# One-core S5/HGRN2/attention trunk: Toeplitz blocks of the S5 layers built through DRAM, weight loads placed by the planner, the taps' copy in a buffer of its own

## The chip, the core and the metric

The kernel runs on one core of a Trainium2 chip. The metric is the device time of one execution in microseconds (us); before the change the median of 3 runs is 1086.48 us (1085.96 to 1090.13).

## The reference, cut to what matters

Four layers run one after the other on x of 512 positions by 1024 features, in float32: S5, HGRN2, sliding-window attention, S5 again. Each is `h = h + rms_norm(branch(rms_norm(h)))`. The change touches only the two S5 layers:

```python
u, z = split(h @ w_in)                       # 1024 -> 2 x 1024
x[l,g,p] = u[l,g,h] * B[g,p,h]               # 64 groups of 16 channels, 64 complex states
s[l] = a * s[l-1] + x[l]                     # associative scan over 512 positions
y = gelu(real(C s) + d * u)
y = y * sigmoid(y @ w_glu + b_glu)
out = (y * silu(z)) @ w_out
```

## The kernel before, in words

**Scan by chunks.** The 512 positions are 64 chunks of 8, the 64 groups are 8 blocks (b = 0 to 7) of 8 groups. For a block `s5_v` makes vt (128x1024) from the parameters prm and the table ap on VectorE, with one factor (q12b) from GpSimd. `s5_taps` multiplies vt with c into kps (the impulse response within a chunk), ScalarE copies kps to kt, TensorE transposes vt (tps, copied to v) and kt (ktp), VectorE adds the skip term and gets ksb. ksb becomes the block's Toeplitz matrix toep: column block jj of it is ksb moved down, with zeros above. `s5_u` brings the projected input of the block through DRAM (ut, ub, u). `s5_core` multiplies u with v (xps), rotates by rotf, scans the 64 chunk states (r), rotates back (spre), and adds u times toep and spre times w into yps; ScalarE takes the gelu (ysb), two transposes (ytp) per pair of blocks bring y back, copied by ScalarE (y).

**Around it.** Between these steps TensorE runs the input projection (`s5_rest`, tile pj, 8 weight chunks), then the first half of the gate projection (`s5_glu_first`, also pj). In the first layer the input weights are used as they are (wraw); every other weight is split on the fly into whi (ScalarE) and wlo (VectorE), two pieces a chunk, and takes three matmuls instead of one. The gate's operand y is split in the same way into yh and yl; yl takes the buffer of the layer's input, so it waits until the input projection is over.

**Order.** `Flow` merges the S5 pieces: each piece says which engine it takes (P, V, A, and D for the SP queue), for how long by a fixed estimate, and after which marks; the earliest start goes next, and the engines then run in that written order. In the first layer, before, the weight loads are not pieces: `w_load` is called where the projection takes a chunk. wraw has 3 buffers, whi and wlo 4 each.

**The shared buffer.** In the first layer kt has the tag of q12b, one buffer: q12b of block b+1 is written after ktp of block b has read kt.

**Opening.** x comes in four loads; `norm_stats` squares and sums a row block on ScalarE, takes the root on GpSimd (rs_r, which needs the constants cst), scales into xs; `norm_xt` transposes (xtp) and copies (xf). `s5_tables` makes the tables of the first layer on VectorE, with sine and cosine on ScalarE.

Of the kernel before, what the change touches and what calls it, by code (L numbers as in the profile page):

```python
# [109 lines left out]
class Trunk:  # L110
# [152 lines left out]
    def norm_stats(self, L, tbs, h):  # L263

        nc = self.nc
        if tbs[0] == 0:
            if L == 0:
                self.x = (self.act.tile([P, KB, T], F32, tag="xh", name="xf"), None)
            else:
                self.x = (  # L270
                    self.act.tile([P, KB, T], F32R, tag="xh", name="xh"),
                    self.act.tile([P, KB, T], F32R, tag="xl", name="xl"),
                )
            self.xs = self.act.tile([P, 4, D], F32, tag="z", name="xs")
        xs = self.xs
        n = len(tbs)
        ss = self.small.tile([P, 2], F32, tag="pre_ss", name="pre_ss", bufs=2)
        for i, tb in enumerate(tbs):
            self.last_sq = nc.scalar.activation(out=xs[:, tb, :], in_=h[:, tb, :], func=AF.Square, accum_out=ss[:, i:i + 1])
        r = self.rstd(ss[:, 0:n], D, n)  # L280
        for i, tb in enumerate(tbs):
            if L == 0:

                nc.scalar.activation(out=xs[:, tb, :], in_=h[:, tb, :], func=AF.Copy, scale=r[:, i:i + 1])
            else:
                self.last_xs = nc.vector.tensor_scalar(out=xs[:, tb, :], in0=h[:, tb, :], scalar1=r[:, i:i + 1], scalar2=None, op0=ALU.mult)
# [336 lines left out]
    def s5_load(self, b, m):  # L623

        nc, s = self.nc, self.scr
        yield "D", 0.2, (m["states", b - 2],) if b > 1 else ()
# [8 lines left out]

    def s5_convs(self, i0, m):

        m["cv", 1].t = 0.0
        for c in range(2, 8):
            yield "A", 2.1, (m["cd", c - 2],) if c > 1 else ()  # L640
            yield "V", 2.6, ()
            self.w_conv(i0 + c)
            self.w_load(i0 + c + 1)
            yield m["cv", c]

    def s5_open(self, j):
# [5 lines left out]
        self.kt = None  # L652
        if j == 0:
            self.s5_params(j)
        else:
            self.s5t = {}
            self.kt = 1
# [6 lines left out]
        self.sp, self.tp, self.cp = [], [], []  # L664
        self.md = s.tile([P, 8, 64], F32, tag="mdec", name="mdec", bufs=1)
        nc.gpsimd.memset(self.md[:, :, 0:1], 0.0)
        for i in range(2):
            t = s.tile([P, 8, 8, 16], F32, tag=f"toep{i}", name="toep", bufs=1)
            nc.gpsimd.memset(t, 0.0)
            self.tp.append(t)  # L670
# [7 lines left out]
    def s5_rot(self, pr, m):  # L678
# [23 lines left out]
        for i in range(2):  # L702

            b = 2 * pr + i
            yield "D", 0.3, (m["states", b - 2],) if pr else ()
# [7 lines left out]
    def s5_v(self, j, b, m):  # L713
# [11 lines left out]
        yield "V", 1.3, (m["ap"],) + ((m["kt", b - 1],) if b and j == 0 else ())  # L725
# [26 lines left out]
    def s5_taps(self, b, m):  # L752
# [11 lines left out]
        kt = self.tab.tile([P, 2, 128], F32, tag="q12b" if self.kt is None else "kt", name="kt", bufs=1)  # L764
# [21 lines left out]
        yield "D", 0.6, (m["y", b - 2],) if b > 1 else ()  # L786
        d["toep"] = toep = self.tp[b % 2]
        for jj in range(8):
            n = (jj + 1) * 16
            nc.sync.dma_start(out=toep[128 - n:128, jj, :, :], in_=ksb[0:n].rearrange("p a g h -> p (a g) h"))  # L790
# [19 lines left out]
    def s5_u(self, b, ps, m):  # L810
# [6 lines left out]
        yield "D", 0.2, ()  # L817
# [3 lines left out]
        yield "D", 0.2, (m["y", b - 3],) if b > 2 else ()  # L821
# [79 lines left out]
    def s5_rest(self, L, ps, m):  # L901
# [5 lines left out]
        def chunk(c):  # L907
            if plain:
                return self.w_next("s5_in")
# [5 lines left out]
        for half in range(2):  # L915
            c = slice(half * 256, half * 256 + 256)
            for b in range(4):
                if half == 0 and b == 2:
                    if not plain:
                        yield "P", 0.0, (m["cv", 1],)  # L920
# [13 lines left out]
        for c in range(6):  # L934
            if not plain:
                yield "P", 0.0, (m["cv", c + 2],)
# [33 lines left out]
    def s5_glu_first(self, glu, y, i0, early, m):  # L970

        w = []
        for c in range(2):
            if early and c == 0:
                yield "A", 2.1, (m["cd", 6],)
                yield "V", 2.6, ()
                self.w_conv(i0 + 8)
                self.w_load(i0 + 9)
                continue
            yield "V", 2.6, (m["rest"],)  # L980
            self.w_conv(self.wi + c)
            self.w_load(self.wi + c + 1)
# [13 lines left out]
        for fb in range(4):  # L996
            if fb == 2:
                yield "V", 2.6, ()
                self.w_conv(self.wi)
                self.w_load(self.wi + 1)  # L1000
# [4 lines left out]
    def layer_s5(self, L):  # L1005
# [6 lines left out]
        with self.scratch("left"), self.tc.manual_schedule(engines={E.PE, E.DVE, E.Activation, E.SP}):  # L1012
# [8 lines left out]
            if j == 0:  # L1021
                flow.add(self.s5_tables(j, m), 0, 5.0)
            else:
# [482 lines left out]
    def run(self):  # L1506
        tc, nc, a = self.tc, self.nc, self.a
        self.plan_weights()
        with tc.tile_pool(name="cst", bufs=1) as self.small, \
# [16 lines left out]
            for tb in range(4):  # L1526
                nc.sync.dma_start(out=x0[:, tb, :], in_=a["x"][tb * 128:(tb + 1) * 128, :])
                if tb == 1:
                    self.w_load(0)
                    self.w_load(1)  # L1530
            for tb in range(4):
                self.norm_stats(self.layers[0], (tb,), x0)
# [128 lines left out]
```

## Time and profile before

| | |
|---|---|
| median of 3 runs | 1086.48 us |
| profiled execution, its own time | 1089.59 us |
| its span | 1087.8 us |
| PE / DVE / ACT / POOL busy | 94% / 69% / 46% / 10% of the span |
| first S5 layer (to the end of the gate projection) | about 0 to 274 us |
| last S5 layer, core blocks | about 858 to 996 us |

PE is TensorE, DVE VectorE, ACT ScalarE, POOL GpSimd, SP the engine that only issues transfers. Busy PE is not PE at its peak: a matmul counts until its modelled end, and the clock that the throttle grants is shown apart. What PE waits for, and at which clock it runs, is read from the timeline by stretches.

### The profile page before, as it was taken

How to read it: one execution, taken by the hardware profiler on the slowest of the kernel's cores; microseconds unless marked ns; L12 is line 12 of the kernel's file. 1: busy time of each engine (PE TensorE's matmuls, PEld its weight loads, DVE VectorE, ACT ScalarE, POOL GpSimd, SP SyncE). 2: the span in 40 equal slices, each digit the busy share in tenths (PEclk: the TensorE clock that was granted, in tenths of full speed). 3: DMA queues.
4: the chain of work that ended last, by engine and by line, in shares of the span. 5: the costliest groups of instructions: out<-in, count | busy, mean ns of one | idle time of the engine just before them, and what ended most of it. 6: DMA issues, size and time to landing. Idle time of an engine off the chain costs nothing.

```text
span 1087.8 us, 17048 instructions
## 1 busy us (share of the span) xinstructions
PE 1027.0 (94%) x6480; PEld 816.6 (75%) x6480; DVE 746.8 (69%) x1454; ACT 505.2 (46%) x937; POOL 104.4 (10%) x164
## 2 busy tenths in 40 slices
PE   5999995999999999999999999999999989897997
PEld 3855554777998798998978986666678867676875
DVE  6487789584689778888865664556656687754752
ACT  5234345554552314323244433588844556555531
POOL 2000000030200100000011021100002111000300
PEclk9999997999999999999999999999999999998999
DMA  6375333434432323424253354211223777634221
GB/s 236 79 207 147 96 102 96 157 112 150 149 106 64 126 83 107 156 73 144 67 188 141 97 134 115 59 58 45 79 83 132 212 189 197 205 96 161 96 97 58
DMA packets 70577, 133.31 MB, mean 123 GB/s; under 512 B 28896, under 2 KB 40032, under 8 KB 69472
## 3 DMA queue, kind: packets, MB, share of 16 engines
q1 hardware_dynamic: 65664, 119.04, 35.5%
q10 hardware_dynamic: 4832, 13.19, 3.7%
q8 instruction: 51, 0.84, 0.3%
q14 instruction: 30, 0.25, 0.1%
HBM read 100.51 MB, written 20.15 MB: 111 GB/s over the span
## 4 chain that ended last, share of the span: by engine, by line
PE 66%; DVE 14%; ACT 7%; DMA 5%; issue 5%; POOL 2%; SPq 2%; ACTq 1%; DVEq 0%; POOLq 0%
PE pj L233 27%; PE ops L248 14%; PE zps L248 4%; PE vps L248 3%; PE sps L1138 3%; DVE wlo L184 3%; PE scps L1346 3%; ACT whi L183 2%; PE aops L1382 2%; DMA rsw<-rraw 1%; PE yps L877 1%; SPq L790 1%; PE yps L875 1%; PE ptp L1377 1%; DVE sg L1067 1%
## 5 line engine op out<-in xcount | busy, mean ns | idle before, releaser
L233 PE MATMUL pj<-xh,whi 128*128 128x512 f32 (+1 forms) x496 | 179.9, 364 | 1.2 <-ACT xh L305 0.6
L184 DVE TENSOR_TENSOR wlo<-wraw,whi 128x1024 fp32r<-128x1024 f32 x116 | 144.6, 1262 | 52.4 <-ACT whi L183 45.2
L233 PE MATMUL pj<-xl,whi 128*128 128x512 f32 (+1 forms) x496 | 175.1, 354 | 2.1 <-DVE xl L311 2.1
L233 PE MATMUL pj<-xh,wlo 128*128 128x512 f32 (+1 forms) x496 | 175.4, 354 | 0.0
L183 ACT ACTIVATE whi<-wraw 128x1024 fp32r<-128x1024 f32 x116 | 120.7, 1056 | 73.2 <-PE pj L233 33.5
L233 PE MATMUL pj<-xf,wraw 128*128 128x512 f32 (+1 forms) x320 | 119.6, 524 | 0.4 <-ACT xf L305 0.4
L233 PEld LDWEIGHTS pj<-xh,whi 128*128 128x128 f32 x496 | 93.8, 190 | 17.5 <-issue 5.4
L233 PEld LDWEIGHTS pj<-xl,whi 128*128 128x128 f32 x496 | 94.4, 190 | 13.9 <-DVE xl L311 2.9
L233 PEld LDWEIGHTS pj<-xh,wlo 128*128 128x128 f32 x496 | 94.2, 190 | 13.5 <-issue 1.7
L248 PE MATMUL ops<-whi,gh 128*128 128x512 f32 x256 | 101.7, 398 | 2.7 <-ACT gh L1069 2.1
L248 PE MATMUL ops<-wlo,gh 128*128 128x512 f32 x256 | 100.7, 394 | 1.1 <-DVE wlo L184 1.0
L248 PE MATMUL ops<-whi,gl 128*128 128x512 f32 x256 | 100.5, 395 | 0.0
L233 PEld LDWEIGHTS pj<-xf,wraw 128*128 128x128 f32 x320 | 61.0, 198 | 42.1 <-issue 36.7
L248 PEld LDWEIGHTS ops<-whi,gh 128*128 128x128 f32 x256 | 48.2, 188 | 13.9 <-ACT gh L1069 3.0
L248 PEld LDWEIGHTS ops<-wlo,gh 128*128 128x128 f32 x256 | 48.2, 188 | 13.1 <-DVE wlo L184 2.7
L248 PEld LDWEIGHTS ops<-whi,gl 128*128 128x128 f32 x256 | 48.1, 188 | 11.2 <-DVE gl L1070 0.9
L233 PE MATMUL pj<-yh,whi 128*128 128x512 f32 x128 | 51.1, 399 | 0.0
L233 PE MATMUL pj<-yh,wlo 128*128 128x512 f32 x128 | 50.1, 392 | 0.0
L233 PE MATMUL pj<-yl,whi 128*128 128x512 f32 x128 | 50.1, 392 | 0.0
L354 DVE TENSOR_TENSOR yg<-ops,gpost 128x512 f32<-128x512 f32 x32 | 21.8, 687 | 38.8 <-ACT junk L352 38.8
L248 PE MATMUL vps<-wlo,xh 128*128 128x256 f32 x160 | 45.3, 283 | 0.0
L248 PE MATMUL vps<-whi,xl 128*128 128x256 f32 x160 | 45.3, 283 | 0.0
(279 smaller groups left out, 2100.4 us busy)
## 6 DMA issues: line engine op xcount, KB each, us to landing
wraw<-in_s_in SPq DMA_DIRECT2D x32, 512.0 KB, 4.7
wraw<-in_hg_in SPq DMA_DIRECT2D x32, 512.0 KB, 3.6
wraw<-in_at_in SPq DMA_DIRECT2D x20, 512.0 KB, 4.3
wraw<-in_s_glu SPq DMA_DIRECT2D x16, 512.0 KB, 3.8
wraw<-in_s_out SPq DMA_DIRECT2D x16, 512.0 KB, 3.5
hd<-h SPq DMA_DIRECT2D x6, 1024.0 KB, 4.0
prm<-in_s_bc SPq DMA_DIRECT2D x16, 256.0 KB, 3.8
ub<-ut SPq DMA_DIRECT2D x16, 256.0 KB, 3.7
```

The lines of the kernel that those rows point to most:

```text
L183: nc.scalar.activation(out=hi, in_=raw, func=AF.Copy)
L184: nc.vector.tensor_tensor(out=lo, in0=raw, in1=hi.bitcast(F32), op=ALU.subtract)
L233: self.nc.tensor.matmul(ps, lhsT=l[k // 4][:, k % 4, c], rhs=r[:, k, n0:n1], start=k == 0 and n == 0, stop=k == KB - 1 and n == len(terms) ...
L248: self.nc.tensor.matmul(ps, lhsT=l[:, k, c], rhs=r[k // per][:, k % per, :], start=k == 0 and n == 0, stop=k == KB - 1 and n == 2)
L354: nc.vector.tensor_tensor(out=yg[:, tb, f], in0=ps, in1=gp[:, f], op=ALU.mult)
L790: nc.sync.dma_start(out=toep[128 - n:128, jj, :, :], in_=ksb[0:n].rearrange("p a g h -> p (a g) h"))
L875: nc.tensor.matmul(o, lhsT=u[:, g, :], rhs=d["toep"][:, :, g, :], start=True, stop=False)
L877: nc.tensor.matmul(o, lhsT=sp[:, g, :], rhs=d["w"][:, g, :], start=False, stop=True)
L1067: nc.vector.tensor_tensor(out=sg, in0=sg, in1=y[:, k, :], op=ALU.mult)
L1138: nc.tensor.matmul(ps[:, c, :], lhsT=k[:, c * 128:c * 128 + 128], rhs=q4[:, c, :, 1, :], start=True, stop=True)
L1346: nc.tensor.matmul(ps[:, bb, lo:256], lhsT=self.q[r, 4 * p + 2 * b2 + bb, qs], rhs=self.k[r, p, ks], start=True, stop=True)
L1382: nc.tensor.matmul(ops[64 * i:64 * i + 64].rearrange("p b q -> p (b q)"), lhsT=self.v[:, n - 1 + f, kv * 64:kv * 64 + 64], rhs=pts[i][:, f ...
```

## The change

Five things change.

1. **toep**: before, eight transfers from ksb to shifted places of one of two tiles that were set to zero once. Now ksb is written once to a DRAM tile kd (240 rows of 128, the first 112 rows zero, written in the opening), and one transfer reads toep from it with overlapping rows. The two zero fills of 128x1024 on GpSimd go; a zero tile of 112x128 and two writes of it on the ACT queue come, ahead of cst.
2. **kt** takes the tag pw in the first layer (a buffer of the tables' making, free by then), and `s5_v` no longer waits for kt of the block before.
3. **Weight loads** become pieces of the planner (`s5_loads` in the first layer, a D piece after each conversion elsewhere), and D pieces have longer estimates.
4. **Opening**: row blocks 0 and 1 share one root, all scaling into xs is on VectorE; the load of chunk 1 is issued after x.
5. All this moves the planner's order in the two S5 layers; the instructions of the two layers between stand in the same order as before.

```diff
         for i, tb in enumerate(tbs):
-            if L == 0:
-
-                nc.scalar.activation(out=xs[:, tb, :], in_=h[:, tb, :], func=AF.Copy, scale=r[:, i:i + 1])
-            else:
-                self.last_xs = nc.vector.tensor_scalar(out=xs[:, tb, :], in0=h[:, tb, :], scalar1=r[:, i:i + 1], scalar2=None, op0=ALU.mult)
+            self.last_xs = nc.vector.tensor_scalar(out=xs[:, tb, :], in0=h[:, tb, :], scalar1=r[:, i:i + 1], scalar2=None, op0=ALU.mult)
 
...
         nc, s = self.nc, self.scr
-        yield "D", 0.2, (m["states", b - 2],) if b > 1 else ()
+        yield "D", 1.1, (m["states", b - 2],) if b > 1 else ()
         f = self.rot[b] = s.tile([P, 2, 512], F32, tag=f"rot{b % 2}", name="rotf", bufs=1)
...
 
+    def s5_loads(self, i0, m):
+
+        for c in range(1, 9):
+            yield "D", 1.0, (m["cd", 6],) if c == 8 else (m["cd", c - 3],) if c > 2 else ()
+            self.w_load(i0 + c)
+            yield m["cv", c]
+
     def s5_convs(self, i0, m):
...
             self.w_conv(i0 + c)
-            self.w_load(i0 + c + 1)
             yield m["cv", c]
+            yield "D", 1.0, ()
+            self.w_load(i0 + c + 1)
 
...
         self.tab = s = self.tabcm.__enter__()
-        self.kt = None
+        self.kt = ("pw", "kt")[j]
         if j == 0:
...
             self.s5t = {}
-            self.kt = 1
             for n, sh in (("ap", [P, 2, 64, 9]), ("co", [P, 2, 2, 64]), ("m8", [P, 64])):
...
             nc.sync.dma_start(out=dm[0:16, :], in_=self.a["s5_d"][j])
-        self.sp, self.tp, self.cp = [], [], []
+        self.sp, self.cp = [], []
+        if j == 0:
+            zero = s.tile([112, 128], F32, tag="t2", name="zero", bufs=1)
+            nc.gpsimd.memset(zero, 0.0)
+            self.kd = []
+            for i in range(2):
+                self.kd.append(self.dram.tile([240, 128], F32, tag=f"kd{i}", name="kd", bufs=1))
+                nc.scalar.dma_start(out=self.kd[i][0:112], in_=zero)
         self.md = s.tile([P, 8, 64], F32, tag="mdec", name="mdec", bufs=1)
...
         for i in range(2):
-            t = s.tile([P, 8, 8, 16], F32, tag=f"toep{i}", name="toep", bufs=1)
-            nc.gpsimd.memset(t, 0.0)
-            self.tp.append(t)
             t = s.tile([P, 8, 64], F32, tag=f"spre{i}", name="spre", bufs=1)
...
             b = 2 * pr + i
-            yield "D", 0.3, (m["states", b - 2],) if pr else ()
+            yield "D", 1.1, (m["states", b - 2],) if pr else ()
             f = s.tile([P, 2, 512], F32, tag=f"rot{i}", name="rotf", bufs=1)
...
         B = prm.rearrange("p k (g h) -> p k g h", h=16)
-        yield "V", 1.3, (m["ap"],) + ((m["kt", b - 1],) if b and j == 0 else ())
+        yield "V", 1.3, (m["ap"],) + ()
         t = self.s5t
...
         yield "A", 0.4, ()
-        kt = self.tab.tile([P, 2, 128], F32, tag="q12b" if self.kt is None else "kt", name="kt", bufs=1)
+        kt = self.tab.tile([P, 2, 128], F32, tag=self.kt, name="kt", bufs=1)
         nc.scalar.activation(out=kt, in_=kps, func=AF.Copy)
...
         nc.vector.tensor_tensor(out=ksb, in0=ktp[:, :, :, 0:16], in1=dmx.rearrange("p (a g) h -> p a g h", a=2), op=ALU.add)
-        yield "D", 0.6, (m["y", b - 2],) if b > 1 else ()
-        d["toep"] = toep = self.tp[b % 2]
-        for jj in range(8):
-            n = (jj + 1) * 16
-            nc.sync.dma_start(out=toep[128 - n:128, jj, :, :], in_=ksb[0:n].rearrange("p a g h -> p (a g) h"))
+        yield "D", 0.5, (m["toep", b - 2],) if b > 1 else ()
+        kd = self.kd[b % 2]
+        nc.sync.dma_start(out=kd[112:240], in_=ksb.rearrange("p a g h -> p (a g h)"))
+        yield "D", 0.5, (m["y", b - 2],) if b > 1 else ()
+        d["toep"] = toep = self.tab.tile([P, 8, 8, 16], F32, tag=f"toep{b % 2}", name="toep", bufs=1)
+
+        src = bass.AP(tensor=kd.tensor, offset=kd.offset, ap=[[128, P], [16 * 128, 8], [1, 128]])
+        nc.sync.dma_start(out=toep.rearrange("p j g h -> p j (g h)"), in_=src)
         yield m["toep", b]
...
         yield m["ev", b]
-        yield "D", 0.2, ()
+        yield "D", 0.5, ()
         ub = self.dram.tile([8, 128, 64], F32, tag="ub", name="ub", bufs=8)
...
         yield m["ub", b]
-        yield "D", 0.2, (m["y", b - 3],) if b > 2 else ()
+        yield "D", 0.5, (m["y", b - 3],) if b > 2 else ()
         u = s.tile([P, 8, 64], F32, tag="u", name="u", bufs=3)
...
             if plain:
-                return self.w_next("s5_in")
+                self.w_conv(self.wi)
             return self.w_take()
...
                 if half == 0 and b == 2:
-                    if not plain:
-                        yield "P", 0.0, (m["cv", 1],)
+                    yield "P", 0.0, (m["cv", 1],)
                     w.append(chunk(1))
...
         for c in range(6):
-            if not plain:
-                yield "P", 0.0, (m["cv", c + 2],)
+            yield "P", 0.0, (m["cv", c + 2],)
             w = chunk(c + 2)
...
                 self.w_conv(i0 + 8)
+                yield "D", 1.0, ()
                 self.w_load(i0 + 9)
...
             yield "V", 2.6, (m["rest"],)
-            self.w_conv(self.wi + c)
-            self.w_load(self.wi + c + 1)
+            self.w_conv(i0 + 8 + c)
+            yield "D", 1.0, ()
+            self.w_load(i0 + 9 + c)
         for c in range(2):
...
                 self.w_conv(self.wi)
+                yield "D", 1.0, ()
                 self.w_load(self.wi + 1)
...
                 flow.add(self.s5_tables(j, m), 0, 5.0)
+                flow.add(self.s5_loads(i0, m), 60)
             else:
...
                     self.w_load(0)
-                    self.w_load(1)
-            for tb in range(4):
-                self.norm_stats(self.layers[0], (tb,), x0)
+            for tbs in ((0, 1), (2,), (3,)):
+                self.norm_stats(self.layers[0], tbs, x0)
             for _ in self.norm_xt(self.layers[0], (0, 1)):
```

**Order on TensorE, first layer, from ktp of block 0 to kps of block 1.** Before:

```order
L779 MATMUL ktp<-cst,kt 128x128 x2
L233 MATMUL pj<-xf,wraw 128x512
L838 MATMUL xps<-u,v 64x64 x16
L233 MATMUL pj<-xf,wraw 128x512 x10
L762 MATMUL kps<-vt,c_92 32x128 x8
```

After:

```order
L786 MATMUL ktp<-cst,kt 128x128 x2
L233 MATMUL pj<-xf,wraw 128x512 x2
L848 MATMUL xps<-u,v 64x64 x16
L233 MATMUL pj<-xf,wraw 128x512 x3
L769 MATMUL kps<-vt,c_94 32x128 x8
L233 MATMUL pj<-xf,wraw 128x512
```

Between the two blocks stood 11 steps of the projection (one of 512 columns each), now 5. So it goes on: the last block's xps, which stood behind the whole projection, now has 8 steps of it behind it, and the yps of blocks 6 and 7 and both ytp follow, before the gate projection.

**Order on ScalarE in the opening**, up to the cosine. Before:

```order
L279 ACTIVATE xs,pre_ss<-x_98 128x1024
L447 ACTIVATE lam<-lam 128x96
L279 ACTIVATE xs,pre_ss<-x_98 128x1024
L454 ACTIVATE mag<-lrdt 128x64
L434 ACT_TABLE_LOAD
L434 ACTIVATE sin<-th 128x96
L437 ACTIVATE cos<-red_n,cst 128x96
L284 ACTIVATE xs<-x_98,rs_r 128x1024 x2
L305 ACTIVATE xf<-xtp,gpre 128x256 x2
```

After:

```order
L279 ACTIVATE xs,pre_ss<-x_100 128x1024 x2
L443 ACTIVATE lam<-lam 128x96
L450 ACTIVATE mag<-lrdt 128x64
L279 ACTIVATE xs,pre_ss<-x_100 128x1024
L301 ACTIVATE xf<-xtp,gpre 128x256 x2
L279 ACTIVATE xs,pre_ss<-x_100 128x1024
L301 ACTIVATE xf<-xtp,gpre 128x256 x4
L430 ACT_TABLE_LOAD
L430 ACTIVATE sin<-th 128x96
L301 ACTIVATE xf<-xtp,gpre 128x256 x2
L433 ACTIVATE cos<-red_n,cst 128x96
```

The scalings have left ScalarE; sine and cosine now stand behind six and eight copies of xf.

**Order on ScalarE at the end of the first layer's projection**, from the gelu of a block's yps (ysb) on; z is the last copy of the projection. Before, from ysb of block 6:

```order
L883 ACTIVATE ysb<-yps 128x4x8x16
L773 ACTIVATE v<-tps 128x512
L183 ACTIVATE whi<-wraw 128x1024 x2
L963 ACTIVATE yh<-y 128x512
L843 ACTIVATE xsw<-xps 64x512
L844 ACTIVATE xsw<-xps 64x512
L856 ACTIVATE rsw<-r 64x512
L857 ACTIVATE rsw<-r 64x512
L883 ACTIVATE ysb<-yps 128x4x8x16
L1065 ACT_TABLE_LOAD
```

After, from ysb of block 6 too:

```order
L893 ACTIVATE ysb<-yps 128x4x8x16
L961 ACTIVATE z<-pj 128x512
L971 ACTIVATE yh<-y 128x512 x2
L183 ACTIVATE whi<-wraw 128x1024 x2
L971 ACTIVATE yh<-y 128x512
L893 ACTIVATE ysb<-yps 128x4x8x16
L1077 ACT_TABLE_LOAD
L1077 ACTIVATE sz<-z 128x512
L906 ACTIVATE y<-ytp 128x4x128 x2
L1502 DMA h<-in_x 128x4x1024
L971 ACTIVATE yh<-y 128x512
L183 ACTIVATE whi<-wraw 128x1024 x2
```

The first whi pair here is the gate's chunk 0, the second its chunk 1. The core steps that stood between (v, xsw, rsw) are over by now, and chunk 1 stands behind both copies of y.

## Rows read from the trace of the kernel before

**Rows 1.** Stretches: length, busy us by engine, clock, DMA share, GB/s

```profile
120.00:160.00 40.00, 39.28 (x255) 21.10 (x254) 30.98 (x40) 16.19 (x27) 2.32 (x4) 1.00 0.37 95
...
160.00:200.00 40.00, 27.89 (x236) 19.95 (x234) 36.24 (x44) 20.37 (x32) 1.35 (x2) 0.83 0.34 92
```

**Rows 2.** Timeline of PE, first layer: start, length, instruction, [idle before]

```profile
20.84 11.03 PE L233 MATMUL pj<-xf,wraw 128*128 128x256 f32 x40 [0.40 <-ACT xf L305]
...
47.22 0.65 PE L762 MATMUL kps<-vt,c 128*32 128x128 f32 x16
...
164.73 0.64 PE L762 MATMUL kps<-vt,c 128*32 128x128 f32 x16
...
183.20 1.08 PE L762 MATMUL kps<-vt,c 128*32 128x128 f32 x16 [9.11 <-DVE vt L748]
...
191.07 0.48 PE L233 MATMUL pj<-yh,whi 128*128 128x512 f32 x1
...
200.96 0.44 PE L875 MATMUL yps<-toep,u 128*64 128x128 f32 x4 [1.43 <-DMA toep<-ksb]
```

**Rows 3.** Projection matmuls (L233) between two kps: stretch, length, PE busy, PEld busy

```profile
125.32:144.98 19.66, 13.39 (x31) 5.47 (x30) 1.00 0.33 81
```

**Rows 4.** Timeline of DVE, first layer

```profile
9.75 0.29 DVE L462 TENSOR_TENSOR ap<-mag,cos 128x64 f32<-128x64 f32 x1 [0.77 <-ACT cos L437]
...
32.43 1.22 DVE L748 TENSOR_TENSOR vt<-vt,t 128x1024 f32<-128x1024 f32 x1
...
54.79 0.29 DVE L785 TENSOR_TENSOR ksb<-ktp,dmx 128x128 f32<-128x128 f32 x1 [9.41 <-PE ktp L779]
```

**Rows 5.** Chain that ended last, its opening: start, length

```profile
1.64 6.95 DMA cst<-in_const
...
10.85 1.14 ACT xs L284
```

**Rows 6.** Line 286: the scaling on VectorE elsewhere, ns min/median/max

```profile
L286 DVE TENSOR_SCALAR xs<-h,rs_r x4: 747/752/1717, 270.2 to 293.9; 128x1024 f32<-128x1024 f32 x4
```

**Rows 7.** Timeline of ACT, first layer

```profile
12.97 0.84 ACT L305 ACTIVATE xf<-xtp,gpre 128x256 f32<-128x256 f32 x2 [0.99 <-PE xtp L301]
...
168.26 0.60 ACT L883 ACTIVATE ysb<-yps 128x512 f32<-128x512 f32 x1 [1.89 <-PE yps L877]
...
169.60 1.11 ACT L896 ACTIVATE y<-ytp 128x512 f32<-128x512 f32 x1 [0.17 <-PE ytp L892]
...
170.50 2.01 ACT L183 ACTIVATE whi<-wraw 128x1024 fp32r<-128x1024 f32 x2
...
203.58 1.28 ACT L1065 ACT_TABLE_LOAD   x1
```

**Rows 8.** PE in one stretch of the last layer: busy, clock

```profile
950.00:954.00 4.00, 3.29 (x21) 0.52 0.43 132
```

**Rows 9.** SP: one block's toep issues; then issues, KB, us to landing

```profile
77.06 5.70 SPq L790 DMA_DIRECT2D toep<-ksb  x8
...
ub<-ut SPq DMA_DIRECT2D x8, 256.0 KB, 3.8
...
u<-ub SPq DMA_DIRECT2D x8, 256.0 KB, 3.1
...
toep<-ksb SPq DMA_DIRECT2D x8, 64.0 KB, 1.9
```

**Rows 10.** Waits of PE, last layer: total, times, longest

```profile
PE yps L877 <- DVE spre L862: 5.2, 2, 4.9
...
PE kps L762 <- DVE vt L748: 3.7, 1, 3.7
...
PE yps L875 <- DMA toep<-ksb: 3.5, 2, 2.7
```

**Rows 11.** Timeline of PE, last layer

```profile
857.53 0.64 PE L762 MATMUL kps<-vt,c 128*32 128x128 f32 x16
...
988.67 0.64 PE L877 MATMUL yps<-w,spre 128*64 128x128 f32 x4
```

More of the change, by code (lines that the diff above doesn't have):

```diff
@@ L642, in s5_convs @@
             self.w_conv(i0 + c)
+            yield m["cv", c]
+            yield "D", 1.0, ()
             self.w_load(i0 + c + 1)
-            yield m["cv", c]
     def s5_open(self, j):
```

## The prediction

> **What bounds the kernel now.** First the busy time by stretches [rows 1]. From 120 to 160 us, inside the first S5 layer, PE is busy for 39.28 of 40 us at full clock: PE itself is the bound there, and nothing that other engines save shows. From 160 to 200 it is busy for only 27.89, at a granted clock of 0.83. So the gain has to come from there, and I read that stretch next, in the timeline of PE [rows 2]. The core of a block begins with kps. From the first kps at 47.22 to the one at 164.73 the projection fills all gaps. There it ends, the last two blocks run alone, the last kps waits 9.11 us for vt, and the gate projection starts at 191.07, with one more wait of 1.43 us for toep at 200.96. How much of the 26.3 us between 164.73 and 191.07 is work: one period of a block, 125.32 to 144.98, holds 13.39 us of projection [rows 3], so a block's own work is 6.3 less a wait of 0.7 in it, 5.6 us. Two blocks are 11.1; the second has no ytp yet, 10.2 remain. 16 us are waits and half clock.
>
> Why the last blocks are so late is in DVE's timeline [rows 4]: ksb at 54.79 waits 9.41 us for ktp, and the q and vt of the next block stand behind it. They wait because q12b of the next block is written into the buffer of kt. So a block begins when ktp of the block before is through, and the blocks can't run ahead, however idle DVE is.
>
> **The opening.** The chain of waits begins with cst, issued at 1.64 and 6.95 us on its way; rs_r needs it, then come the ACT scalings of 1.14 each [rows 5]. After the change the scalings run on DVE, at 0.75 [rows 6]; ACT keeps two of its four sums between the xf copies and no scaling. First xf before: 12.97 [rows 7]; projection without a gap from 20.84, 7.9 us later [rows 2].
>
> After: cst is issued behind two writes of zeros, some 0.9 us later. With its landing as before it arrives at 9.5. GpSimd's steps behind it took 1.1 (cst at 8.6, the second scaling at 10.85, the first 1.14) and take some 1.3 now that both root steps stand behind dmx; two scalings are 1.5; from the last scaling to the first xf it was 1.0: first xf at 13.3. From there ACT needs 0.84 (two xf), 1.2 (a sum, reckoned like the scaling of the same size) and 1.6 (four xf), and PE, which no longer waits for scalings between, runs without a gap from its fifth projection step, about 5.1 us after the first xf: 18.4 against 20.84, a gain of 2.4. Should cst come at 8 (fewer weights are ahead of it), the sums bound it, first xf is at 11.4 and the gain is 4.4. I take 3.0: the first kps at 44.2.
>
> The Trainium skill, "DMA: Bandwidth & Descriptors", section "Queues, rings and completion order", says that each DMA engine goes round the queues that have work, a packet at a time. By that the zeros ahead of cst on ACT's queue cost more than their issue: 112 KB against the some 350 KB of lam and cst would, as an estimate, put off its landing by another 1.6 us, and the gain would be 1.0 to 1.4. No row shows which holds; cst's 6.95 us beside the x loads do show a queue that shares.
>
> The cost of the new ACT order: sine and cosine stand behind six and eight xf copies. Table load, sine, two xf and cosine end about 6.4 us after the first xf, at 19.6, where before DVE took up the tables at 9.75. From there to the end of the first vt it was 23.9 us (32.43 plus 1.22) [rows 4]; so vt is ready at 43.5, just ahead of PE at 44.2. I cost it at nothing; the cover is 0.7 us, and a later cosine moves kps by as much.
>
> **The blocks of the first layer.** Work of PE from the first kps to the end of the first gate part, without the gate's matmuls: 117.5 less 0.7 to 164.73, 10.2 for two blocks, 2.6 for the last yps and ytp, 129.6. Before it took 143.85 to 191.07, plus 1.43 and 2.6: 147.9. In the new order kps of block 1 has 5 projection steps ahead of it since ktp, not 11, and its vt no longer needs ktp: vt1 stands right behind ksb0, three DVE instructions of 1.22 against 5.4 us of PE (five steps of 0.86, two records each [rows 3], and xps). DVE's load per block is 30.98 of 40 us [rows 1], 15.2 in a period of 19.66, so 122 for eight, inside PE's 125 to the end of the projection; I put 3 us for small waits (0 to 6), as in places ACT's y copies take 1.11 [rows 7] where the planner reckons 0.6.
>
> What is left is the passage to the gate projection. When the projection ends (R), PE has two yps (3.8 us), then ytp, which waits for the last ysb. On ACT this stands behind ysb, z, three yh and two whi. By their rows [rows 7]: 1.9 (first yps) + 0.6 + 0.6 + 1.2 + 2.0 + 0.6 + 0.6, so ytp at R + 7.5; then 1.28 for the table load, 0.6 sz (sz and yh reckoned like ysb), 2.2 two y, 0.6 yh, 1.0 whi of chunk 1, 1.2 its wlo (as vt, the same size): R + 14.4. PE has 6.5 us of work in that time (3.8, 0.9 ytp, 1.9 for 8 gate matmuls), 8.0 are idle. A clock that has fallen costs 2.3 on top: in the last layer a wait of 3.67 us was followed by 4 us at 0.52, which is the 1.2 GHz level [rows 8]. After: 129.6 + 3 + 8.0 + 2.3 = 142.9, a gain of 5.0; with the opening 8.0.
>
> **toep and the queue.** Eight issues occupy SP for 5.70 us, and the last lands 1.9 later: 7.6 [rows 9]. The new path is one write into DRAM and one read, in turn, with SP waiting between: nearest rows 3.8 (ub<-ut) and 3.1 (u<-ub, 1024 pieces too, of half the size), with issues 7.9; upper bound two landings like cst, 14.9, lower bound two like the small toep piece, 4.8. I take 7.9: no gain in itself. Between ktp and yps of a block the new order leaves PE 12 to 14 us of work, so it is covered; SP is free 4.6 us more per block. The two zero fills on GpSimd were not on the path: nothing.
>
> **The last layer.** kt had its own buffer here, so only the new order acts. Waits of PE from 840 to 1000: 5.2 for spre, 3.7 for vt, 3.5 for toep [rows 10]; from the first kps at 857.53 to the end of the last yps at 989.3 it is 131.8 us [rows 11]. In the new order 24 matmuls, not 3, stand ahead of yps of block 1, and prm of the next block is issued ahead of the weight load: the 2.7 for toep and the 3.67 for vt go, with the slow clock behind the latter, about 9 us. New: ahead of xps of block 5 ACT has two y (2.2), two rsw (1.3), two whi (2.0), mdec and v (1.2), PE some 3.1 of transposes and projection beside them, 3.6 to wait, in block 6 likewise 2.0, with some slow clock; the last spre keeps two wlo ahead of it and waits 4.0 rather than 5.8. Net 3.5, bounds -3 and +9.
>
> **Sum.** 3.0 + 5.0 + 3.5 = 11.5. The profiled execution took 1089.59 us (span 1087.8), so 1078.1 for such a one; it was 3.1 above the median of the runs, 1086.48, so 1075.0 on that scale.
>
> **Rivals.** (B) PE never waits: the passage is hidden, since by then yh, whi and ysb are done earlier than I chain them. Opening 4.4, first layer 147.9 - 129.6 = 18.3, last layer 3.5: 1060.3. For it: ACT is busy for 16.19 of 40 us in the middle of that layer [rows 1]; against: its written order.
> (C) The gain is given back: the tables come late. If cosine is 3 us later, the first kps is at 46.5 or later, DVE's 120 us then end close to R, the last spre too, and PE waits for it at R as it does now for vt. Opening 0.5, first layer 2, last layer 0: 1084.0. For it: a cover of only 0.7 us.
> (D) Slower: toep decides. From two landings of together more than 12 us on, yps waits in each block, and TensorE falls to half clock. At 14.9 it is 2.9 late in each of the eight blocks of the last layer, where SP also carries all split weights, 23 us, and the gain of the first layer is halved: 1086.5 + 23 - 4 = 1105. For it: SP waits for the first landing with the next loads behind it; against: before, ub and u take the same way through DRAM in 6.9 us.
> (E) The change doesn't do what it says: the blocks come forward in the written order, but PE waits for vt or v in each, since ACT carries more than planned. 16 blocks of 0.7 eat the 11.5: 1086.5.
>
> **How the numbers follow.** Forecast 0.55, B 0.13, C 0.14, D 0.09, E 0.09. The forecast's own range, from its bounds (opening 1.0 to 4.4, small waits 0 to 6, passage 5 to 11, last layer -3 to +9), is 1065 to 1083. The range for 8 in 10 is 1062 to 1087: it leaves out D, half of B and some of E. A change of under 0.5% (5.4 us: 1081.0 to 1091.9) is what a measurement can't tell from none. Faster: 0.52 of the forecast, 0.13 B, half of C and a third of E, 0.75; same: 0.03, the other half of C, two thirds of E, 0.16; slower: D, 0.09.
>
> **What would show it.** In the profile after: kps of block 1 some 14 us after that of block 0, not 18.2; no wait of kps for vt in the first layer; R at about 173 and, behind it, PE idle for about 8 us with ytp waiting for ysb and the gate for whi or wlo; first kps at 44.2, its vt at 43.5; toep about 8 us after ksb, with no wait of yps for it; in the last layer waits of xps for v. Wrong would be: kps late in the middle of the first layer (C, E), yps waiting for toep (D), a gate that starts without a gap (B).

## The result, and the profile after

The changed kernel takes 1070.19 us (median, 1068.02 to 1070.83), the kernel before 1086.22 beside it: ratio 0.9837, 95% interval 0.9819 to 0.9854, faster by 16.0 us by the medians and 17.7 by the ratio. Measured again, beside later experiments, it was 1069.16 against 1087.93, ratio 0.9831 (0.9811 to 0.9851). The two profiled executions lie further apart, 1089.59 and 1068.02 us (span 1066.2), since that of before is 3.4 us over its median and that of after 2.2 under.

PE's timeline of the changed kernel in the first layer (start, length, instruction, idle before it) answers to [rows 2]:

```profile
17.52 9.23 PE L233 MATMUL pj<-xf,wraw 128*128 128x256 f32 x42
...
43.01 0.65 PE L769 MATMUL kps<-vt,c 128*32 128x128 f32 x16 [0.83 <-DVE vt L755]
...
162.72 7.03 PE L233 MATMUL pj<-xf,wraw 128*128 128x512 f32 x16
...
172.35 0.44 PE L885 MATMUL yps<-toep,u 128*64 128x128 f32 x4 [0.70 <-ACT ysb L893]
...
176.77 1.22 PE L902 MATMUL ytp<-cst,ysb 128*128 128x128 f32 x8 [2.45 <-ACT ysb L893]
177.64 0.78 PE L233 MATMUL pj<-yh,whi 128*128 128x512 f32 x1
...
182.25 0.50 PE L233 MATMUL pj<-yh,whi 128*128 128x512 f32 x1 [1.70 <-ACT whi L183]
...
226.98 0.39 PE L248 MATMUL ops<-whi,gh 128*128 128x512 f32 x1
```

The first kps comes 4.2 us earlier. The projection ends at 169.7, with all eight blocks begun: the wait of 9.11 for vt is gone. In its place come short waits on ACT. ACT's timeline in that passage shows why:

```profile
173.71 2.00 ACT L183 ACTIVATE whi<-wraw 128x1024 fp32r<-128x1024 f32 x2
175.60 0.63 ACT L971 ACTIVATE yh<-y 128x512 fp32r<-128x512 f32 x1
176.12 0.59 ACT L893 ACTIVATE ysb<-yps 128x512 f32<-128x512 f32 x1
176.73 1.28 ACT L1077 ACT_TABLE_LOAD   x1
178.03 0.63 ACT L1077 ACTIVATE sz<-z 128x512 f32<-128x512 f32 x1
...
178.56 2.03 ACT L906 ACTIVATE y<-ytp 128x512 f32<-128x512 f32 x2
180.62 0.63 ACT L971 ACTIVATE yh<-y 128x512 fp32r<-128x512 f32 x1
181.16 1.99 ACT L183 ACTIVATE whi<-wraw 128x1024 fp32r<-128x1024 f32 x2
```

ysb stands behind the first gate chunk's whi, and the second chunk's whi (181.16) behind y. PE waits for both. Of the signs that the prediction names, kps of block 1 comes 13.0 us after that of block 0 (forecast 14), and the one of no wait of kps for vt fails by the 0.83 above.

The waits of PE in the last layer (total, times, longest) answer to [rows 10]:

```profile
PE yps L887 <- DVE spre L872: 4.8, 2, 4.6
PE xps L848 <- ACT v L780: 3.4, 3, 1.6
PE tps L778 <- ACT y L906: 0.7, 1, 0.7
PE ytp L902 <- ACT y L906: 0.6, 1, 0.6
PE yps L885 <- DMA toep<-kd: 0.4, 1, 0.4
```

vt is gone and toep nearly so; xps now waits for v, as forecast.

Most runs below are read by one table, made from the timelines: the first kps, the time from there to the first ops (output projection), and the same for the last layer, in us. Runs on different chips are compared by their ratios to the kernel before beside them: it took 1088.35 beside the first four experiments, 1087.93 beside the next four, 1088.20 beside the last four. a2_after is the changed kernel again.

| kernel | median | first kps | first layer | between | last layer |
|---|---|---|---|---|---|
| before | 1086.22 | 47.22 | 192.1 | 618.2 | 177.2 |
| after | 1070.19 | 43.01 | 184.0 | 616.5 | 169.9 |
| a2_after | 1069.16 | 42.70 | 184.6 | 618.7 | 170.4 |
| e1 kt shared | 1079.42 | 42.78 | 194.7 | 617.3 | 170.3 |
| e2 kt alone | 1078.21 | 46.59 | 184.4 | 616.3 | 176.8 |
| e3 toep in eight | 1077.60 | 42.22 | 188.9 | 616.3 | 172.5 |
| e4 old opening | 1071.48 | 46.35 | 184.0 | 616.3 | 172.3 |
| e4b, the same | 1072.90 | 46.16 | 184.0 | 615.8 | 169.9 |
| e5 old loads | 1064.34 | 42.67 | 179.3 | 616.4 | 170.2 |
| e6 zeros late | 1069.22 | 42.58 | 183.6 | 617.9 | 170.3 |
| e13 gate loads inline | 1066.44 | 42.35 | 179.0 | 618.2 | 171.8 |
| e10 old loads, states first | 1061.89 | 42.41 | 179.9 | 617.2 | 168.3 |
| e17 and first chunk early | 1060.51 | 42.91 | 177.5 | 616.7 | 168.8 |

"Between" is the same work in all of them and moves by up to 2.9 us from run to run (615.8 to 618.7); a difference of that size in one trace proves nothing. The same holds for the last layer up to 2.4 us: e4 and e4b are one kernel, with 172.3 and 169.9. One execution, the profiled one of e7, took 2020 us, as TensorE's matmuls took nearly twice their time throughout (the float32 projection's 961 ns on the mean for 516) while its granted clock reads 1.00, so it is left out and e7 has no row.

### The profile page after: what moved, and what is told of

Same layout as the page of the kernel before. It is cut to its first block, busy times and chain, and to the rows that moved or that the text cites. A ratio compares the mean times of both kernels' runs of the same rounds, so it can differ in the third digit from the quotient of the medians.

```text
span 1066.2 us, 16860 instructions
## 1 busy us (share of the span) xinstructions
PE 1017.2 (95%) x6480; PEld 810.4 (76%) x6480; DVE 750.0 (70%) x1458; ACT 499.6 (47%) x933; POOL 104.4 (10%) x159
## 4 chain that ended last, share of the span: by engine, by line
PE 76%; DVE 10%; ACT 5%; issue 3%; DMA 3%; POOL 1%; ACTq 1%; DVEq 0%; POOLq 0%; SPq 0%
PE pj L233 34%; PE ops L248 15%; PE zps L248 5%; PE vps L248 3%; PE sps L1150 3%; PE scps L1358 2%; DVE wlo L184 2%; PE aops L1394 2%; PE xps L848 1%; DMA rsw<-rraw 1%; PE yps L885 1%; PE yps L887 1%; PE ptp L1389 1%; ACT whi L183 1%; PE tps L778 1%
## 5 line engine op out<-in xcount | busy, mean ns | idle before, releaser
L233 PE MATMUL pj<-xh,whi 128*128 128x512 f32 (+1 forms) x496 | 178.6, 362 | 0.8 <-ACT xh L301 0.6
L233 PE MATMUL pj<-xl,whi 128*128 128x512 f32 (+1 forms) x496 | 174.2, 352 | 1.3 <-DVE xl L307 1.3
L233 PE MATMUL pj<-xh,wlo 128*128 128x512 f32 (+1 forms) x496 | 174.7, 353 | 0.0
L233 PE MATMUL pj<-xf,wraw 128*128 128x512 f32 (+1 forms) x320 | 119.7, 516 | 0.1
L233 PEld LDWEIGHTS pj<-xh,whi 128*128 128x128 f32 x496 | 93.5, 189 | 16.7 <-issue 4.9
L233 PEld LDWEIGHTS pj<-xh,wlo 128*128 128x128 f32 x496 | 93.9, 189 | 13.4 <-issue 1.7
L233 PEld LDWEIGHTS pj<-xl,whi 128*128 128x128 f32 x496 | 94.0, 189 | 13.0 <-DVE xl L307 1.9
L233 PEld LDWEIGHTS pj<-xf,wraw 128*128 128x128 f32 x320 | 58.2, 193 | 34.8 <-issue 30.9
L233 PE MATMUL pj<-yh,whi 128*128 128x512 f32 x128 | 51.9, 405 | 1.7 <-ACT whi L183 1.7
L233 PE MATMUL pj<-yh,wlo 128*128 128x512 f32 x128 | 51.2, 400 | 0.5 <-DVE wlo L184 0.5
L233 PE MATMUL pj<-yl,whi 128*128 128x512 f32 x128 | 51.1, 400 | 0.0
```

What stands on the lines that cost most here:

```text
L233: self.nc.tensor.matmul(ps, lhsT=l[k // 4][:, k % 4, c], rhs=r[:, k, n0:n1], start=k == 0 and n == 0, stop=k == KB - 1 and n == len(terms) ...
```

## The experiments

**e1 and e2: the buffer of kt.** e1 takes it back, e2 makes it alone in the kernel before.

```diff
-        self.kt = ("pw", "kt")[j]
+        self.kt = ("q12b", "kt")[j]
...
-        yield "V", 1.3, (m["ap"],) + ()
+        yield "V", 1.3, (m["ap"],) + ((m["kt", b - 1],) if b and j == 0 else ())
```

> The changed kernel, but kt shares the buffer of q12b again in the first layer and the step of the next block waits for it. K (kt's buffer carries the gain of the first layer after the opening, 8.2 us by the two profiles): the last kps of the first layer waits for vt again, PE falls to half clock behind it, the gate projection of that layer ends about 8 us later, the last layer as in the changed kernel; about 1078 us. T (the freed SP queue and the single toep transfer carry it): within 2 us of the changed kernel, 1070 to 1072.

> The kernel before with one edit: kt has a buffer of its own in the first layer and the step of the next block no longer waits for it. K: no wait of the last kps for vt, the gate projection of the first layer starts behind the input projection; 6 to 8 us faster than before, about 1079, the opening and the last layer as before. T: SP still issues eight transfers of toep per block, 5 us, and blocks that come closer together find toep late; waits of yps for toep eat the gain, about 1085.

e1 1079.42, ratio 0.9924 (0.9897 to 0.9951); e2 1078.21, ratio 0.9909 (0.9876 to 0.9943). Alone the buffer gives 10.1 us, more than the 6 to 8 expected; without it 9.2 of the whole gain are gone (9.5 by the ratios). The first layer carries it: 184.4 with the buffer alone for 192.1, 194.7 with all but the buffer, where the old wait is back:

```profile
PE kps L769 <- DVE vt L755: 10.2, 2, 9.1
```

**e3: toep in eight transfers**, into zeroed tiles as before; all else as changed.

```diff
-        nc.sync.dma_start(out=kd[112:240], in_=ksb.rearrange("p a g h -> p (a g h)"))
...
-        nc.sync.dma_start(out=toep.rearrange("p j g h -> p j (g h)"), in_=src)
+        yield "D", 0.6, (m["y", b - 2],) if b > 1 else ()
+        d["toep"] = toep = self.tp[b % 2]
+        for jj in range(8):
+            n = (jj + 1) * 16
+            nc.sync.dma_start(out=toep[128 - n:128, jj, :, :], in_=ksb[0:n].rearrange("p a g h -> p (a g) h"))
```

> The changed kernel with toep made by eight transfers into zeroed tiles again, everything else as changed. K: the first layer stays within 2 us; of the 7.3 us of the last layer some 3 go (yps waits for toep again, as before 2.7 and 0.8); about 1073. T: the gains of both layers go, 1080 or more.

1077.60, ratio 0.9901 (0.9871 to 0.9932): 7.4 us of the gain are gone by the medians, 7.0 by the ratios, between what the two theories had. But not the transfer alone was taken back: with other D pieces the planner also makes another order on PE and DVE. The first layer is 4.9 us longer, mostly at one place, the yps of the last block, which waits for toep:

```profile
168.67 4.46 PE L233 MATMUL pj<-xf,wraw 128*128 128x512 f32 x10
...
178.17 0.70 PE L878 MATMUL yps<-toep,u 128*64 128x128 f32 x4 [5.05 <-DMA toep<-ksb]
```

```profile
171.24 0.26 DVE L788 TENSOR_TENSOR ksb<-ktp,dmx 128x128 f32<-128x128 f32 x1
```

```profile
171.53 5.01 SPq L793 DMA_DIRECT2D toep<-ksb  x8
```

From the end of ksb to that yps it is 6.7 us; write and read in the changed kernel take 5.9 (below). So the path is only 0.8 longer. The rest is order: ksb stands behind four steps of the block's scan and ends 2.7 us after ktp, not 0.4; and behind ktp stand 10 records of the projection, 4.46 us, not the 16 of 7.03. In the order of the changed kernel ksb is over at 163.26 and that yps starts at 172.35, so that by these numbers, as an estimate, eight transfers would have been in time. No run has them in that order.

In the last layer the wait that returns is the 3.7 for vt and not the one for toep (0.8):

```profile
PE kps L765 <- DVE vt L751: 4.0, 2, 3.7
```

Ahead of it SP issues prm behind eight toep issues, and DVE waits 3.03 us for prm; in the changed kernel it waits 1.44 there. That this is what brings the 3.7 is argued and not shown.

In the changed kernel, whose columns are issues, KB and median us to landing, the read is one:

```profile
toep<-kd SPq DMA_DIRECT2D x4, 512.0 KB, 4.3
```

Write issued at 163.29, read at 164.91, landed some 4.3 later: 5.9 us in all, under the 7.9 of the forecast and far from the 12 of rival D.

**e4 and e4b: the old opening** in the changed kernel (the second time beside the changed kernel).

```diff
-            for tbs in ((0, 1), (2,), (3,)):
-                self.norm_stats(self.layers[0], tbs, x0)
+                    self.w_load(1)
+            for tb in range(4):
+                self.norm_stats(self.layers[0], (tb,), x0)
...
+            if L == 0:
+                nc.scalar.activation(out=xs[:, tb, :], in_=h[:, tb, :], func=AF.Copy, scale=r[:, i:i + 1])
```

> The changed kernel with the opening of before: scalings on ScalarE, one root per row block, chunk 1 loaded ahead of the last two x. If the opening's 4.2 us come from the scalings and sums: first kps at 47, about 1074. If they come from elsewhere (tables of the planner, weight loads): within 1 us of the changed kernel. In the profile the projection matmuls behind the transposes should take twice their time until about 25 us, as before, and not until 17 us only.

> The changed kernel with the opening of before (a sum for each block of tokens, its scaling on ACT, the second weight load ahead of x2). By the profiles the first kps came 3.3 us later with it (46.35 against 43.01) and nothing behind it gave that back by the first ops. Theory O, the opening's gain reaches the end: 3 to 4 us slower than the changed kernel. Rival, the gain is given back or is one profile's luck: under 1.5 us slower.

1071.48, ratio 0.9849 (0.9819 to 0.9880), which could not tell; then 1072.90 against 1069.16, ratio 0.9867 (0.9850 to 0.9884): 3.7 us, and both traces have the first kps 3.3 to 3.5 later. Theory O holds for the price. But it isn't paid as in the kernel before. The matmuls that were expected to take twice their time until about 25 us take 379 ns, nearly all of them, from about 16.5 us on, and what makes the first kps late is vt, whose tables wait for the cosine. In e4b:

```profile
21.75 0.37 ACT L436 ACTIVATE cos<-red_n,cst 128x96 f32<-128x96 f32 x1
```

```profile
46.16 0.64 PE L772 MATMUL kps<-vt,c 128*32 128x128 f32 x16 [1.16 <-DVE vt L758]
```

Before, the cosine stood ahead of the scalings (DVE took up the tables at 9.75 [rows 4]); in this order it stands behind them and all copies of xf. In the changed kernel it is 3.2 us earlier, at 18.59, and so is the first kps, which waits for vt there too. So e4 prices the old scalings in the new order of ACT; no run has the whole opening of before in the changed kernel.

Between the kernels before and after the traces give another account. ACT's rows after show what the 4.2 us don't come from:

```profile
11.86 1.06 ACT L279 ACTIVATE xs<-x 128x1024 f32<-128x1024 f32 x1 [2.96 <-DMA x<-in_x]
...
12.92 0.82 ACT L301 ACTIVATE xf<-xtp,gpre 128x256 f32<-128x256 f32 x2
...
18.59 0.37 ACT L433 ACTIVATE cos<-red_n,cst 128x96 f32<-128x96 f32 x1
```

The first xf is where it was (12.97 before [rows 7]); ACT waits for x2 now. What changed is that PE's steps have no gaps between them, so that the run without a gap starts at 17.52, with one step more to do, for 20.84 [rows 2]: 2.9 us. And its rate: 42 records in 9.23 us after, 40 in 11.03 before, another 2.2; the wait for vt takes 0.83 of it back. The granted clock reads 1.00 for both, though a matmul takes 634 ns before until about 25 us and 379 after; in the kernel with kt's buffer alone, whose opening is that of before and which took 10.30 us for 40, the clock shows (stretch, length, PE busy, clock, DMA share, GB/s):

```profile
20.00:22.00 2.00, 1.05 (x3) 0.60 0.04 2
22.00:24.00 2.00, 2.00 (x7) 0.55 0.00 0
```

After the gaps of 1.35 and 1.21 us in its projection TensorE works near its lower level, 1.2 GHz, until 24 us. Gaps alone don't do it: those of e4b, 1.11 and 1.40, left it at 379 ns, but there the matmuls had come to that rate ahead of the gaps (8 in 1.89 us from 16.44), here not yet (4 in 1.73 from 15.56). So 2.2 of the 5.1 us between before and after go with that rate; e4, which has no such stretch, loses 3.3 to 3.5 all the same, to the late cosine.

**e6: the zeros behind the constants** on ACT's queue.

```diff
-                nc.scalar.dma_start(out=self.kd[i][0:112], in_=zero)
+                self.kdz = zero
...
             nc.scalar.dma_start(out=self.gpre, in_=a["norm_pre"])
+            for i in range(2):
+                nc.scalar.dma_start(out=self.kd[i][0:112], in_=self.kdz)
```

> The changed kernel with the two zero writes to DRAM issued behind the constants and gains on ACT's queue. If transfers that are under way together share the engines packet by packet, the constants land up to 1.6 us earlier (at 7.1 in place of 8.7), rs_r follows, and the first xf comes 0.7 to 1.6 us earlier. Rival, what the trace of the changed kernel shows (constants 5.9 us on their way with the zero writes ahead of them, landing 0.1 us later than before): constants at 8.4 to 8.8, first xf within 0.3 us of 12.9, total within 0.5 us.

1069.22, ratio 0.9833 (0.9817 to 0.9848): as the changed kernel. Issued at 1.64 in place of 2.80, the constants are 6.7 us on their way and land at 8.3; in the changed kernel:

```profile
cst<-in_const ACTq DMA_DIRECT2D x1, 206.0 KB, 5.9
```

That is 8.7, as before the change (1.64 and 6.95, [rows 5]). The first xf is at 12.48, 0.4 earlier, but in the second run of the unmoved kernel it is at 12.51. In the nine traces with the zeros ahead the constants land at 8.2 to 8.9, in the four without at 8.3 to 9.0: the zeros delay nothing that can be measured. By the rule that I cited from the Trainium skill ("DMA: Bandwidth & Descriptors", "Queues, rings and completion order"), each DMA engine going round the queues with work a packet at a time, they would, as an estimate, have put the constants off by 1.6 us. These traces don't agree with that estimate. The rule may hold and the packets of the zeros be cheap: that was not separated.

**e5: the loads as before**, with the planner's old costs of transfers.

```diff
-        yield "D", 1.1, (m["states", b - 2],) if b > 1 else ()
+        yield "D", 0.2, (m["states", b - 2],) if b > 1 else ()
...
             self.w_conv(i0 + 8 + c)
-            yield "D", 1.0, ()
             self.w_load(i0 + 9 + c)
...
-                flow.add(self.s5_loads(i0, m), 60)
```

> The changed kernel with weight loads issued with their conversion as before and the planner's old costs for transfers; the buffer for kt, the one transfer and the opening stay. In the last layer the kernel with only kt's buffer took 176.8 us from the first kps to the first ops, the one with all but the one transfer 172.5, the changed one 169.9. Theory L, the joint order of the loads is worth those 4.3 us: last layer 173 to 175, total 3 to 5 us over the changed kernel. Rival, it is the one transfer with whatever order: last layer 170 to 171, total within 1 us.

1064.34, ratio 0.9789 (0.9770 to 0.9807). Theory L fell, and the rival with it: the last layer is 170.2, as the rival had it, but the total is 4.8 us *less*. So one part of the change cost time. It is in the first layer (179.3 for 184.6).

**e13: only the gate's loads inline**, the line `yield "D", 1.0, ()` between a gate chunk's conversion and the next load taken out in its three places.

> The changed kernel with one line taken back: the loads of the gate's chunks stand with the conversion ahead of them again and are no pieces of their own in the joint order; all else as changed. Theory G, the 4.8 us that the old loads gave are the passage to the gate in the first layer, where these pieces put the second chunk's whi behind y's copies on ACT: first ops of the first layer 4 to 5.5 us earlier (222 to 223), total 1064 to 1065. Rival, it is the input chunks' loads or the planner's costs: first ops at 226 to 228, total within 1 us of the changed kernel.

1066.44, ratio 0.9802 (0.9788 to 0.9815). Theory G holds for the first layer: first ops at 221.33, and on ACT the second chunk's whi stand ahead of y:

```profile
175.46 0.59 ACT L893 ACTIVATE ysb<-yps 128x512 f32<-128x512 f32 x1
175.94 1.06 ACT L183 ACTIVATE whi<-wraw 128x1024 fp32r<-128x1024 f32 x1
177.02 1.28 ACT L1074 ACT_TABLE_LOAD   x1
178.31 0.63 ACT L1074 ACTIVATE sz<-z 128x512 f32<-128x512 f32 x1
178.94 1.06 ACT L183 ACTIVATE whi<-wraw 128x1024 fp32r<-128x1024 f32 x1
...
179.91 2.22 ACT L906 ACTIVATE y<-ytp 128x512 f32<-128x512 f32 x2
```

The gate's 1.70 us of waiting for whi are gone, and PE, idle for less, gets through 37 records between 182 and 190 us at a clock of 1.00, where the changed kernel has 23 at 0.79 (below; stretch, length, busy us of PE, PEld, DVE, ACT, POOL, clock, DMA share, GB/s):

```profile
182.00:190.00 8.00, 8.00 (x37) 6.64 (x36) 2.76 (x4) 3.68 (x6) 0.00 (x0) 1.00 0.92 342
```

The total is 1.4 us above the forecast since the same line did good in the last layer. There SP now takes the gate's load ahead of the last toep, and that load waits for a buffer; SP's rows, then PE's:

```profile
950.48 0.33 SPq L795 DMA_DIRECT2D kd<-ksb  x1
950.90 7.35 SPq L153 DMA_DIRECT2D wraw<-in_s_glu  x2
958.30 0.43 SPq L800 DMA_DIRECT2D toep<-kd  x1
```

```profile
963.05 0.70 PE L885 MATMUL yps<-toep,u 128*64 128x128 f32 x4 [7.49 <-DMA toep<-kd]
```

It takes the place of the 4.60 us for spre, so only 1.4 to 1.9 us are lost, no more than one kernel's traces differ by.

**e7: the last block's states ahead of the gate's second chunk**, last layer only (`early` is true there).

```diff
-            yield "V", 2.6, (m["rest"],)
+            yield "V", 2.6, (m["rest"], m["states", 7]) if early else (m["rest"],)
```

> The changed kernel, in the last layer only: the conversion of the gate's second weight chunk (two whi on ACT, two wlo on DVE) waits in the planner for the last block's states, so that rsw, r and spre come ahead of it. Theory: the 4.6 us in which the last yps waits for spre is 3.4 us of those wlo and the matmuls at half the clock behind it are 1.3 more; last layer from the first kps to the first ops 165 to 167 in place of 170, total 3 to 5 us less than the changed kernel (1065 to 1066). Rival, the two whi are then late for the gate: last layer 169 to 171, total within 1 us.

1067.67, ratio 0.9811 (0.9796 to 0.9825): by the ratios 2.2 us under the changed kernel, whose interval overlaps this one, and less than the 3 to 5 of the theory. No trace shows which waits changed. Not settled by itself.

**e10 and e17: a better version.** e10 is e5 with the edit of e7; e17 also converts the gate's first chunk before the projection ends.

```diff
-            if early and c == 0:
+            if c == 0:
+                if not early:
+                    yield "D", 1.0, (m["cd", 6],)
                 yield "A", 2.1, (m["cd", 6],)
```

> The changed kernel with the old weight loads and costs and, in the last layer, the last block's states ahead of the gate's second chunk. Theory, both gains add: the wait of 5.4 us for yl in the last layer falls under 2, last layer 166 to 168, total 1060 to 1062. Rival, the gate's whi is late instead: last layer 169 to 171, total 1064.

> The kernel of old loads and states first, and the gate's first weight chunk converted in the first layer before the projection has ended, so that the last ysb on ACT does not stand behind it and the gate's matmuls fill the time in which PE waits for the last block (0.7 and 2.5 us, and matmuls at half the clock after them). Theory: first layer 3 to 5 us less, total 1056 to 1059. Rival, the conversion of 2 us on ACT ahead of xsw delays the last block by as much, or the second chunk's load is not there in time: within 1 us of the kernel without it, or slower.

e10 1061.89, ratio 0.9763 (0.9748 to 0.9778): 2.4 less than e5, with overlapping intervals; the total is as forecast, the wait for yl is gone, the last layer is at the edge of the forecast. e17 1060.51, ratio 0.9752 (0.9737 to 0.9767), above the 1056 to 1059 of its theory; its first layer gains 2.4 rather than 3 to 5, as the waits for ysb go and a new one for yl comes:

```profile
PE pj L233 <- DVE yl L976: 2.0, 1, 2.0
```

By time e17 is 1.4 us under e10, with overlapping intervals; both are clearly under the changed kernel, by 7 to 9 us.

## Why the prediction was right, and where its sizes were off

The forecast was 1075.0 (1062 to 1087), faster; measured 1070.19. By traces its three terms were 3.0 + 5.0 + 3.5 = 11.5 and came to 4.2 + 8.2 + 7.3 = 19.7. By the ratios of runs with one part taken back, the buffer is worth 9.5, the one transfer with its order 7.0, the opening 3.9, the loads -4.6, each to within 3 or 4 us: together 15.8, beside 17.7 for the whole, though parts that stand in for each other (below) need not add. That the total fell into the range is in part luck: all three terms were too small, and the cost of the loads, which was no term, made up for some of it. The forecast's own range of 1065 to 1083 is also narrower than its bounds added up, 1062 to 1089.5.

- *Opening* (3.0 forecast, 3.7 by time): the size came out, the way only in part. "First xf at 13.3" was 12.92, held by the sum of x2 and not by the constants, "runs without a gap from 18.4" 17.52. Not counted was the rate: before, the projection ran slowly behind its gaps. PE would have been at kps at 42.2, but vt sets its start: cosine over at 18.96 (forecast 19.6), plus 23.9. The cover for vt (0.7), which I put at nothing, was gone, and kps waits 0.83.
- *The blocks* (small waits 3): 0.33 and 0.56 us. DVE, freed of the wait for ktp (26.3 us of this layer before, 2.6 after), was ahead nearly everywhere. This is 2.1 of the 3.2 us missing in the first layer's term.
- *Passage to the gate* (R + 14.4, 8.0 idle, 2.3 for the clock): R + 13.8, 5.4 idle (0.70, 2.45, 1.70 and 0.53), so the chain on ACT was read rightly, instruction by instruction. The clock cost as much as forecast or more, 2.5 us by the windows of this execution (columns as in e13):

```profile
178.00:182.00 4.00, 2.55 (x6) 1.44 (x5) 0.96 (x2) 3.96 (x6) 1.37 (x1) 0.62 0.94 273
182.00:190.00 8.00, 7.23 (x23) 5.48 (x24) 4.64 (x4) 2.19 (x4) 1.46 (x1) 0.79 0.92 363
```

  and 3.9 by those of the second run of the kernel:

```profile
178.00:182.00 4.00, 1.93 (x6) 1.01 (x4) 0.75 (x3) 3.97 (x6) 1.37 (x1) 0.50 0.98 309
182.00:190.00 8.00, 7.96 (x22) 5.87 (x23) 4.55 (x4) 1.86 (x3) 1.47 (x1) 0.63 0.84 335
```

  There 1.93 us at half the clock lose 1.0, 7.96 at 0.63 lose 2.9. What I didn't see is that a piece of the change itself put whi of the second chunk at the end of that chain; I took this order as given, and its price, 5.0 to 5.6 us of the first layer, was never a term.
- *toep* (7.9, covered, no gain in itself): 5.9, and covered. As to the length of the path the step holds: in e3 the old one is 0.8 longer. "No gain" was the step that failed, for I took the order as given: with eight transfers the planner makes one in which the last block leaves less time between ksb and yps (5.05 of waiting in e3) and prm comes late in the last layer, and 7.0 us hang on transfer and order together. What the transfer is worth in one and the same order stays open.
- *Last layer* (3.5, bounds -3 and +9): 7.3. The waits for v that I put at 3.6 and 2.0 were 1.61 and 0.58, with one of 1.24 more, and left no slow clock behind; spre 4.60 for 4.0. Which part brings the gain: the one transfer with old loads 170.2, the new loads with eight transfers 172.5, neither 176.8. Each alone brings most of it, as far as single traces tell. The one transfer takes the 3.7 for vt away, with old loads too; with the new loads alone that wait stays and the one for toep falls from 2.7 to 0.8.

Of the rivals, C had half a point (kps does wait for vt), but DVE made it up; in e4, with the cosine 3.2 us later, the first kps comes at 46.2 to 46.4, close to C's 46.5, and the rest of C doesn't follow. B's 1060.3 is what e17 reaches, by other means: the passage has to be emptied by order, it does not empty itself. D, toep behind a blocked SP, appears in e13; lesser waits for the one transfer are in e1 (2.6) and e17 (2.1).

## What to carry to other kernels

When a planner's pieces are moved, price each move by itself on the in-order engine where it lands: here one line, in three places, cost 5 us in one layer and, as far as one trace tells, saved 1.4 to 1.9 in another. A transfer that is hidden in the old order must be set against the cover in the new one. A part that is taken back in the changed kernel and one that is made alone in the old answer different questions; where two parts remove the same wait, only both tell. And where a planner orders the whole, a part taken back moves the order of the rest, so read from the trace which wait its price was paid in.

## What was not expected of the hardware

The granted clock of a stretch can read 1.00 while matmuls take much longer: in the opening of before 128x256 ones took 554 to 796 ns until about 25 us, most of them 634, and 379 after, and another run of the same opening shows 0.55 to 0.60 between 20 and 24 us. A read of 512 KB from DRAM in one transfer landed 4.3 us after its issue, where eight issues alone held SP for 5.0 to 5.7.
